# Seven block products in place of eight, extended from seven gate and up blocks to an eighth and to part of the down projection

## The chip, the core and the metric

The kernel runs on one core of a Trainium2 chip. The core has five engines that run side by side and wait for each other through semaphores: TensorE (PE in the profile; its weight loads are PEld), VectorE (DVE), ScalarE (ACT), GpSimd (POOL) and SyncE (SP), which issues most of the transfers from HBM. The metric is the device time of one execution in microseconds (us). What must be the same after a change is the output, within the reference's tolerance; weights come in float32.

## The reference, cut to what matters

256 tokens of width 2048 pass one layer: a mixer, a cross-attention to 256 memory tokens, and a feed-forward network of width 5632. The change lies in the last one and in the norm behind it:

```python
def swiglu(h, w_gate, w_up, w_down):
    return (jax.nn.silu(h @ w_gate) * (h @ w_up)) @ w_down
...
        h = h + swiglu(rmsnorm(h, norm_ffn[i]), w_gate[i], w_up[i], w_down[i])
    return rmsnorm(h, norm_final)
```

`w_gate` and `w_up` are 2048 x 5632, `w_down` is 5632 x 2048.

## The kernel before, in words

**Every product is three matmuls.** A float32 operand is split into a high part that TensorE's fp32r format holds exactly and the low rest: `h` is written by a cast on ScalarE (L208), `l` by a subtraction on VectorE (L209). A product is then high x high, low x high (both with the weight's `h`; L282 and L283) and high x low (L286), summed in PSUM. The tokens (or features) are the stationary operand, 128 x 128; the weights stream by, 128 x 512.

**The weights are one long stream.** `stream_plan` lists keys, and each key is a 256 x 512 block of a weight matrix, laid out as 128 x 1024 (two halves of 512 columns, one for each of two feature tiles). `load_to` has SP load the next key into one of six raw buffers `r`; `split_to` makes `h` and `l` (four buffers each); `tok_mm` multiplies. A key used in the plain way ("plain key") is 2 feature tiles x 2 token halves = 4 block products of three matmuls: 12 matmuls, first eight with `h`, then four with `l`. `unit` sets the order written by hand on PE and SP: it loads up to six keys ahead, splits up to three ahead, runs the matmuls, and appends a list of generators (`post`) that evacuate and go on step by step. VectorE, ScalarE and GpSimd are ordered by the tile scheduler.

**Gate and up, in 11 column blocks of 512** (`ffn_units`). Block 0, and blocks 8 to 10, use the plain way. In blocks 1 to 7 (`SEVEN`) two of the eight key pairs, ("g", n, c) and ("u", n, c) with c of 0 and 1, are multiplied together: two feature tiles by two token halves on one side, two feature tiles by gate and up columns on the other are a 2 x 2 by 2 x 2 block product. Done plainly that is eight block products; `seven_mm` does it with seven (Winograd's form), 21 matmuls in place of 24. It needs

- sums of weight blocks, `pair_sums`: four additions on VectorE in float32 (L182 to L185) and then the split of three new blocks of 128 x 512 (cast L189, subtraction L190);
- sums of token blocks, `token_sums`, made once for c of 0 and 1 and used by all seven blocks;
- four extra PSUM accumulators `p` (tag `m`), whose results `p_post` combines into four corrections (L1080 to L1083), and which `whole` adds to the gate and up accumulators (tag `a`, L1094).

`g_post` applies SiLU on ScalarE, `u_post` multiplies (L1111), transposes (L301) and takes the block through DRAM and back (`put`, `get`, both on SP's queue), after which it is split and kept in `gs` as the features of the down projection. There are 22 such feature pairs, two tiles of 128 each.

**The down projection** takes the four output column blocks n in turn, each with 22 plain keys ("d", n, c). The last two keys of a block (four of the last) are ordered by token half, so that `d_evac` (L1208 and L1211) on the first half runs beside the matmuls of the second.

**Buffers**: `slot` has 63 buffers of 128 x 512 for whatever lives long; `tmp` eight of 128 x 256; `feat` (tag `f`) three of 128 x 1024, used by `get` and `p_post`; `gate` four of 128 x 512.

Of the kernel before, what the change touches and what calls it, by code (L numbers as in the profile page):

```python
# [28 lines left out]
SEVEN = range(1, 8)  # L30
# [55 lines left out]
def ffn_order():  # L86

    return [k for u in ffn_units() for part in u for k in part]


def stream_plan():
# [8 lines left out]
    p += [(k, 1024) for k in ffn_order()]  # L100
    for n in range(4):
        p += [(("d", n, c), 1024) for c in range(FT // 2)]
# [3 lines left out]
def trunk(tc, wst, vecs, xp, xtp, mp, mtp, wdt_in, nfin, outp):  # L106
# [9 lines left out]
    with ExitStack() as ctx:  # L116
# [57 lines left out]
        pairs = {k for u in ffn_units() for part in u if len(part) == 2 for k in part}  # L174

        def pair_sums(nc_, u):


            g = held.pop(nc_)
# [6 lines left out]
            pair_parts[nc_] = []  # L186
            for x in (f[:, a], f[:, b], g[:, a]):
                h, l = slot(dt=F32R), slot(dt=F32R)
                nc.scalar.copy(h, x)  # L189
                tt(l, x, h.bitcast(F32), ALU.subtract)  # L190
                pair_parts[nc_].append((h, l))

        def split_to(n):
            while nsplit[0] < min(n, len(plan)):
# [3 lines left out]
                if key in pairs:  # L198
                    if key[0] == "g":
                        held[key[1:]] = r  # L200
                    else:
                        pair_sums(key[1:], r)
# [872 lines left out]
        def p_post(n, p):  # L1075
# [9 lines left out]
                       ("u", 0): (c12, ALU.add), ("u", 1): (c22, ALU.add)}  # L1085
            return
# [40 lines left out]
        def token_sums(c):  # L1127

            s0, s1 = h2g[2 * c], h2g[2 * c + 1]
            x, y = slot(), slot()  # L1130
            for i, a in enumerate((s0, s1)):
                tt(x[:, i * T:i * T + T], a[:, 0:T].bitcast(F32), a[:, T:].bitcast(F32), ALU.add)
            a11, a21, a12, a22 = [x[:, i * 128:i * 128 + 128] for i in range(4)]
            o = [y[:, i * 128:i * 128 + 128] for i in range(4)]
# [4 lines left out]
            h, l = slot(dt=F32R), slot(dt=F32R)  # L1139
            nc.scalar.copy(h, y)  # L1140
            tt(l, y, h.bitcast(F32), ALU.subtract)
            seven_a[c] = [(h[:, i * 128:i * 128 + 128], l[:, i * 128:i * 128 + 128]) for i in range(4)]

        def seven_mm(n, c):

            g, u, p = faccs["g", n], faccs["u", n], shared[n]
            gh, gl = fin(("g", n, c))
            uh, ul = fin(("u", n, c))
            t1, t2, t4 = pair_parts.pop((n, c))
            a, b = slice(0, 512), slice(512, 1024)  # L1150
            raw = side_blocks(h2g, 2 * c)
            sa = seven_a[c]
            for group in (((p[0], raw(0, 0), (gh[:, a], gl[:, a])), (g[0], raw(1, 0), (gh[:, b], gl[:, b]))),
                          ((p[3], sa[2], (uh[:, a], ul[:, a])), (p[1], sa[0], t1)),
                          ((p[2], sa[1], t2), (g[1], raw(1, 1), t4), (u[0], sa[3], (uh[:, b], ul[:, b])))):
                for ps, (ah, al), (bh, bl) in group:
                    mm(ps, ah, bh, start=c == 0, stop=False)  # L1157
                    mm(ps, al, bh, start=False, stop=False)  # L1158
                for ps, (ah, al), (bh, bl) in group:
                    mm(ps, ah, bl, start=False, stop=c == 1 and any(ps is q for q in p))  # L1160

        def part_mm(part):
            m, n, c = part[0]
            if len(part) == 2:
                seven_mm(n, c)
# [6 lines left out]
        for i, parts in enumerate(ffn_units()):  # L1172
            if i == 8:
                for c in range(2):
                    token_sums(c)
# [26 lines left out]
        for n in range(4):  # L1202
            before.setdefault(index[("d", 0, 8 + 2 * n)], []).append(lambda n=n: load_gain(n))

        def d_evac(n, tb, ps):
# [3 lines left out]
            j = slot()  # L1209
# [12 lines left out]
        def d_sums(tb, ps):  # L1222
            h, j = res[tb][3], slot()
# [58 lines left out]
        nd = FT // 2  # L1282
        for n in range(4):
            accs = [acc(), acc()]
            nt = 2 if n < 3 else 4
            for c in range(0, nd - nt, 2):
                unit([([("d", n, k)], lambda k=k: d_mm(accs, ("d", n, k), (0, 1), k == 0, False))
                      for k in (c, c + 1)])
            tail = [("d", n, k) for k in range(nd - nt, nd)]

            def last_mm(tb):
# [141 lines left out]
```

## Time and profile before

| | |
|---|---|
| median of 3 runs | 1500.95 us (1500.62 to 1501.08) |
| the profiled execution: its time, and the span from its first to its last instruction | 1500.12 us, 1498.4 us |
| busy, share of the span: PE, PEld, DVE, ACT, POOL | 99%, 82%, 68%, 53%, 2% |
| mean granted TensorE clock | 0.998 |
| DMA, mean over the span | 231 GB/s |

The profiled execution's time holds 1.72 us around its span, and it lies 0.83 us below the median of the runs. A row of the timeline gives the start, the length, the engine, the source line, the operation, the tiles (written <- read) and in brackets how long the engine had been idle and what ended that. Lengths of instructions that follow each other overlap, above all on PE, so that the distance between two starts is what an instruction takes of a full engine.

### The profile page before, as it was taken

How to read it: one execution, taken by the hardware profiler on the slowest of the kernel's cores; microseconds unless marked ns; L12 is line 12 of the kernel's file. 1: busy time of each engine (PE TensorE's matmuls, PEld its weight loads, DVE VectorE, ACT ScalarE, POOL GpSimd, SP SyncE). 2: the span in 40 equal slices, each digit the busy share in tenths (PEclk: the TensorE clock that was granted, in tenths of full speed). 3: DMA queues.
4: the chain of work that ended last, by engine and by line, in shares of the span. 5: the costliest groups of instructions: out<-in, count | busy, mean ns of one | idle time of the engine just before them, and what ended most of it. 6: DMA issues, size and time to landing. Idle time of an engine off the chain costs nothing.

```text
span 1498.4 us, 18385 instructions
## 1 busy us (share of the span) xinstructions
PE 1488.0 (99%) x6691; PEld 1226.5 (82%) x6691; DVE 1016.0 (68%) x1320; ACT 796.3 (53%) x1084; POOL 35.3 (2%) x46
## 2 busy tenths in 40 slices
PE   9999999999999999999999999999999999999997
PEld 7788888888888888888888888888888888888886
DVE  6677676777785765665578888888875555445453
ACT  7477554857654544555465555555554444444343
POOL 0011000101000000000000000000000000000000
PEclk9999999999999999999999999999999999999999
DMA  9786766868766766876656766666567667566652
GB/s 367 264 292 224 270 234 212 291 220 291 265 215 240 253 212 210 279 263 207 249 183 228 245 231 225 222 225 223 207 217 243 221 225 248 187 197 196 196 192 90
DMA packets 149211, 346.69 MB, mean 231 GB/s; under 512 B 11360, under 2 KB 62976, under 8 KB 149120
## 3 DMA queue, kind: packets, MB, share of 16 engines
q1 hardware_dynamic: 140064, 338.64, 65.7%
q10 hardware_dynamic: 9056, 6.87, 1.5%
q8 instruction: 52, 0.85, 0.2%
q14 instruction: 39, 0.32, 0.1%
HBM read 321.30 MB, written 24.17 MB: 231 GB/s over the span
## 4 chain that ended last, share of the span: by engine, by line
PE 99%; issue 0%; DMA 0%; SPq 0%; ACT 0%; DVE 0%; DVEq 0%; POOLq 0%; POOL 0%
PE a L282 30%; PE a L283 30%; PE a L286 30%; PE m L1157 1%; PE m L1160 1%; PE m L1158 1%; PE a L1158 1%; PE a L1160 1%; PE a L1157 1%; PE m L703 1%; PE m L283 0%; PE m L286 0%; PE m L282 0%; DMA r<-in_w_dram 0%; PE m L1010 0%
## 5 line engine op out<-in xcount | busy, mean ns | idle before, releaser
L209 DVE TENSOR_TENSOR l<-r,h 128x1024 fp32r<-128x1024 f32 (+1 forms) x539 | 653.6, 1219 | 365.0 <-ACT h L208 355.6
L208 ACT CAST h<-r 128x1024 fp32r<-128x1024 f32 (+1 forms) x539 | 563.1, 1048 | 546.7 <-PE a L283 456.3
L282 PE MATMUL a<-h,s 128*128 128x512 f32 x1999 | 781.9, 391 | 0.2 <-ACT h L208 0.2
L283 PE MATMUL a<-h,s 128*128 128x512 f32 x1999 | 778.1, 389 | 0.0
L286 PE MATMUL a<-l,s 128*128 128x512 f32 x1999 | 538.0, 389 | 0.0
L282 PEld LDWEIGHTS a<-h,s 128*128 128x128 f32 x1999 | 375.4, 188 | 80.2 <-issue 2.0
L286 PEld LDWEIGHTS a<-l,s 128*128 128x128 f32 x1999 | 375.2, 188 | 78.2
L283 PEld LDWEIGHTS a<-h,s 128*128 128x128 f32 x1999 | 375.4, 188 | 77.0
L301 DVE STREAM_TRANSPOSE b<-s 128x512 f32<-128x512 f32 x62 | 40.6, 689 | 6.7 <-ACT s L308 6.7
L644 DVE SCALAR_TENSOR_TENSOR t<-t,vec,t 128x255 f32<-128x255 f32 (+2 forms) x72 | 33.1, 491 | 4.2 <-ACT t L641 3.5
L308 ACT ACTIVATE s<-a,xr 128x512 f32<-128x512 f32 x42 | 26.4, 681 | 4.0 <-PE a L286 4.0
L1094 DVE TENSOR_TENSOR f<-a,f 128x512 f32<-128x512 f32 x28 | 18.0, 684 | 7.8 <-PE a L286 7.8
L1121 ACT CAST s<-f 128x512 fp32r<-128x512 f32 x22 | 13.2, 619 | 14.9 <-DMA f<-w 14.9
L189 ACT CAST s<-b 128x512 fp32r<-128x512 f32 x28 | 16.7, 617 | 4.5 <-DVE b L182 3.6
L190 DVE TENSOR_TENSOR s<-b,s 128x512 fp32r<-128x512 f32 x28 | 18.7, 684 | 0.0
L223 DVE SCALAR_TENSOR_TENSOR s<-s,vec,s 128x256 fp32r<-128x256 f32 x32 | 14.5, 480 | 5.5 <-ACT s L222 5.5
L1233 POOL TENSOR_TENSOR fr<-fr,half 128x1 f32<-128x1 f32 x2 | 1.1, 552 | 704.9 <-DVE fr L1232 704.9
L1122 DVE TENSOR_TENSOR s<-f,s 128x512 fp32r<-128x512 f32 x22 | 14.9, 687 | 3.9 <-ACT s L1121 3.0
L182 DVE TENSOR_TENSOR b<-r,r 128x512 f32<-128x512 f32 x14 | 9.7, 690 | 11.0 <-DMA r<-in_w_dram 11.0
L262 POOL TENSOR_TENSOR rr<-rv,half 128x2 f32<-128x2 f32 x8 | 6.5, 813 | 409.6 <-DVE rv L261 409.6
L626 ACT ACTIVATE s<-s,nacs 128x256 f32<-128x256 f32 x32 | 16.1, 502 | 0.0
L222 ACT ACTIVATE s<-s,vec 128x256 fp32r<-128x256 f32 x32 | 15.2, 502 | 0.8 <-DMA vec<-in_v_dram 0.6
(218 smaller groups left out, 774.9 us busy)
## 6 DMA issues: line engine op xcount, KB each, us to landing
r<-in_w_dram SPq DMA_DIRECT2D x535, 512.0 KB, 4.4
w<-b SPq DMA_DIRECT2D x42, 512.0 KB, 3.3
f<-w SPq DMA_DIRECT2D x42, 512.0 KB, 5.0
s<-acsT ACTq DMA_DIRECT2D x24, 256.0 KB, 4.9
s<-in_xt_dram SPq DMA_DIRECT2D x16, 256.0 KB, 7.2
s<-in_mt_dram SPq DMA_DIRECT2D x8, 256.0 KB, 6.3
s<-in_m_dram SPq DMA_DIRECT2D x8, 256.0 KB, 4.2
s<-in_x_dram SPq DMA_DIRECT2D x7, 256.0 KB, 7.4
```

The lines of the kernel that those rows point to most:

```text
L190: tt(l, x, h.bitcast(F32), ALU.subtract)
L208: nc.scalar.copy(h[:, c], r[:, c])
L209: tt(l[:, c], r[:, c], h[:, c].bitcast(F32), ALU.subtract)
L282: mm(ps[tb], ah, h[:, w], start=first and i == ks[0], stop=False)
L283: mm(ps[tb], al, h[:, w], start=False, stop=False)
L286: mm(ps[tb], blocks(i, tb)[0], l[:, i * 512:i * 512 + 512], start=False, stop=stop and i == ks[-1])
L301: nc.vector.transpose(t[:, tb * 512:tb * 512 + 512], src[tb])
L308: act(o[tb], accs[tb], AF.Identity, scale=r[:, tb:tb + 1])
L644: stt(a[:, d:], u[:, 0:T - d], v("cw", 4 * ct + k), a[:, d:], ALU.mult, ALU.add)
L1157: mm(ps, ah, bh, start=c == 0, stop=False)
L1158: mm(ps, al, bh, start=False, stop=False)
L1160: mm(ps, ah, bl, start=False, stop=c == 1 and any(ps is q for q in p))
```

## The change

`SEVEN` now runs to block 8. In the down projection two column blocks, n and n + 1, are taken together, first 0 and 1, then 2 and 3: the keys ("d", n, c) and ("d", n + 1, c) of the feature pairs c of 0 to 5 are multiplied by `seven_mm`, with the features of pair c as the one side and the two column blocks as the other; the other 16 feature pairs stay plain. Between the pairs stand plain keys by the list `GAPS`: two ahead of the first pair, then 4, 5, 4, 5 and 4. The token sums of a feature pair are made for each of the two column pairs anew, now with buffers of `feat` and `tmp` in place of `slot`. The corrections of the down projection are added to the residual stream in `p_post`. The scratch of the squares (`j`) goes from `slot` to `gate`, and the four loads of the last norm's gain move by one key.

The diff, cut to its core (what is renamed only, and how one function hands its arguments to the next, is left out):

```diff
-SEVEN = range(1, 8)
+SEVEN = range(1, 9)
+GAPS = (2, 4, 5, 4, 5, 4)
...
+def down_units():
+    o = []
+    for n in (0, 2):
+        q = len(GAPS)
+        plain = [("d", n + i, c) for i in range(2) for c in range(q, FT // 2)]
+        tail = 2 if n == 0 else 4
+        for c, k in enumerate(GAPS):
+            o += [[(a,) for a in plain[i:min(i + 2, k)]] for i in range(0, k, 2)]
+            del plain[:k]
+            o.append([(("d", n, c), ("d", n + 1, c))])
+        o += [[(a,) for a in plain[i:min(i + 2, len(plain) - tail)]] for i in range(0, len(plain) - tail, 2)]
+        o.append([(a,) for a in plain[-tail:]])
+    return o
...
-        def p_post(n, p):
+        def p_post(n, p, first=None):
...
+            if n == "d":
+                for i, m in enumerate("gu"):
+                    for tb in range(2):
+                        c, op = corr[n][m, tb]
+                        h = res[tb][first + i]
+                        tt(h, h, c, op)
...
-        def token_sums(c):
-            s0, s1 = h2g[2 * c], h2g[2 * c + 1]
-            x, y = slot(), slot()
-            for i, a in enumerate((s0, s1)):
-                tt(x[:, i * T:i * T + T], a[:, 0:T].bitcast(F32), a[:, T:].bitcast(F32), ALU.add)
...
+        def token_sums(key, parts):
+            xy = fp.tile([128, 1024], F32, tag="f", name=nm("f"))
+            w = 512 // len(parts)
+            for i, (hi, lo) in enumerate(parts):
+                tt(xy[:, i * w:i * w + w], hi.bitcast(F32), lo.bitcast(F32), ALU.add)
+            a11, a21, a12, a22, *o = [xy[:, i * 128:i * 128 + 128] for i in range(8)]
             tt(o[0], a21, a22, ALU.subtract)
             tt(o[1], a11, o[0], ALU.subtract)
             tt(o[2], a21, a11, ALU.subtract)
             tt(o[3], a12, o[1], ALU.subtract)
-            h, l = slot(dt=F32R), slot(dt=F32R)
-            nc.scalar.copy(h, y)
-            tt(l, y, h.bitcast(F32), ALU.subtract)
...
+            for i in range(2):
+                h, l = [tp.tile([128, T], F32R, tag="t", name=nm("t")) for _ in range(2)]
+                y = xy[:, 512 + i * T:512 + i * T + T]
+                nc.scalar.copy(h, y)
+                tt(l, y, h.bitcast(F32), ALU.subtract)
...
         for i, parts in enumerate(ffn_units()):
+            if i == len(ffn_units()) - 3:
+                token_sums(("d", 0, 0), [gs[0]])
...
-            j = slot()
+            j = gtp.tile([128, 512], F32, tag="g", name=nm("j"))
...
-        for n in range(4):
-            accs = [acc(), acc()]
-            nt = 2 if n < 3 else 4
-            for c in range(0, nd - nt, 2):
-                unit([([("d", n, k)], lambda k=k: d_mm(accs, ("d", n, k), (0, 1), k == 0, False))
-                      for k in (c, c + 1)])
...
+        for i, parts in enumerate(units):
+            for key in sums_at.get(i, []):
+                token_sums(key, [gs[key[2]]])
...
+            if len(parts[0]) == 2:
+                _, n, c = keys[0]
+                if c == 0:
+                    shared["d", n] = [msc() for _ in range(4)]
+                if c == len(GAPS) - 1:
+                    post = [p_post("d", shared["d", n], n), d_post(n, daccs[n])]
```

The changed file's lines stand 16 to 26 further down: the split of a key is L224 (cast) and L225 (subtraction) there, the sums of weight blocks L199 to L202 with the splits L206 and L207, `u_post` L1133 and the transposes L317, the matmuls of a plain key L298, L299 and L302, those of `seven_mm` L1179, L1180 and L1182, the token sums L1155 to L1160 with the splits L1165 and L1166, and `d_evac` L1234 and L1237.

Three places show how the orders change. On **TensorE** in the down projection, one plain key of column block 0 before (12 rows for 4 block products: `a_10758` and `a_10759` are the two token halves), and of the change the last 9 of the 21 rows of a pair (c of 1, column blocks 0 and 1; `m_` is an accumulator of `p`, `t_` a token sum, `s_11011` to `s_11020` are weight sums, `s_7487` and `s_7488` the high and low features):

```order
L282 MATMUL a_10758<-h_10857,s_8545 128x512
L283 MATMUL a_10758<-h_10857,s_8546 128x512
L282 MATMUL a_10759<-h_10857,s_8545 128x512
L283 MATMUL a_10759<-h_10857,s_8546 128x512
L282 MATMUL a_10758<-h_10857,s_8545 128x512
L283 MATMUL a_10758<-h_10857,s_8546 128x512
L282 MATMUL a_10759<-h_10857,s_8545 128x512
L283 MATMUL a_10759<-h_10857,s_8546 128x512
L286 MATMUL a_10758<-l_10858,s_8545 128x512
L286 MATMUL a_10759<-l_10858,s_8545 128x512
L286 MATMUL a_10758<-l_10858,s_8545 128x512
L286 MATMUL a_10759<-l_10858,s_8545 128x512
```

The rows of the change are these:

```order
L1179 MATMUL m_10887<-s_11015,t_10932 128x512
L1180 MATMUL m_10887<-s_11015,t_10933 128x512
L1179 MATMUL a_10822<-s_11019,s_7487 128x512
L1180 MATMUL a_10822<-s_11019,s_7488 128x512
L1179 MATMUL a_10883<-h_11023,t_10936 128x512
L1180 MATMUL a_10883<-h_11023,t_10937 128x512
L1182 MATMUL m_10887<-s_11016,t_10932 128x512
L1182 MATMUL a_10822<-s_11020,s_7487 128x512
L1182 MATMUL a_10883<-l_11024,t_10936 128x512
```

Two plain keys (24 matmuls) have become one pair with 21, three for each of seven block products, and the pair reads weight sums and token sums beside the keys themselves. Over the whole program the change has 42 matmuls fewer: 3 for each of 14 pairs, two in block 8 and twelve in the down projection.

On **VectorE** at the seam between gate and up and the down projection, before (`l_10780` to `l_10822` are splits of plain keys; `g_10621` and `g_10623` the last gate and up block, `b_10776` its transpose):

```order
L209 TENSOR_TENSOR l_10780<-r_10717,h_10779 128x1024
L1111 SCALAR_TENSOR_TENSOR g_10621<-a_10605,fscale,g_10621 128x512
L1111 SCALAR_TENSOR_TENSOR g_10623<-a_10606,fscale,g_10623 128x512
L301 STREAM_TRANSPOSE b_10776<-g_10621 128x512
L301 STREAM_TRANSPOSE b_10776<-g_10623 128x512
L209 TENSOR_TENSOR l_10784<-r_10719,h_10783 128x1024
L209 TENSOR_TENSOR l_10818<-r_10753,h_10817 128x1024
L209 TENSOR_TENSOR l_10822<-r_10760,h_10821 128x1024
```

And of the change, at the same place (`l_10801` is the second plain key ahead of the first pair, `r_10780` and `r_10782` are the raw keys of that pair, `l_10845` and `l_10866` their splits):

```order
L225 TENSOR_TENSOR l_10845<-r_10780,h_10844 128x1024
L1133 SCALAR_TENSOR_TENSOR g_10670<-a_10654,fscale,g_10670 128x512
L1133 SCALAR_TENSOR_TENSOR g_10672<-a_10655,fscale,g_10672 128x512
L317 STREAM_TRANSPOSE b_10841<-g_10670 128x512
L317 STREAM_TRANSPOSE b_10841<-g_10672 128x512
L199 TENSOR_TENSOR b_10848<-r_10780,r_10782 128x512
L200 TENSOR_TENSOR r_10782<-r_10782 128x512
L201 TENSOR_TENSOR b_10848<-b_10848,r_10782 128x512
L207 TENSOR_TENSOR s_10854<-b_10848,s_10853 128x512
L202 TENSOR_TENSOR r_10780<-b_10848,r_10780 128x512
L207 TENSOR_TENSOR s_10858<-b_10848,s_10857 128x512
L225 TENSOR_TENSOR l_10866<-r_10782,h_10865 128x1024
```

The sums of the first pair now stand behind `u_post` and ahead of the split of the pair's second key.

On **SP** at the start of the feed-forward network, where the features come back from DRAM (`w_7100` is the last quarter of them, `f_7174` before and `f_7180` now its buffer; the brackets name the semaphores that the issue waits for, DMAHW of a transfer, DVE of VectorE), before:

```order
L321 DMA f_7098<-w_7060 128x8x128 [waits DMAHW4_49,DMAHW1_49]
L314 DMA w_7100<-b_6969 128x2x512 [waits DMAHW5_49]
L169 DMA r_7106<-in_w_dram 128x1024 [waits DMAHW6_49,DVE_49]
L169 DMA r_7136<-in_w_dram 128x1024 [waits DMAHW7_49,DVE_49]
L321 DMA f_7174<-w_7100 128x8x128 [waits DMAHW5_49,DMAHW0_49]
```

And of the change:

```order
L337 DMA f_7098<-w_7060 128x8x128 [waits DMAHW4_49,DMAHW1_49]
L330 DMA w_7100<-b_6969 128x2x512 [waits DMAHW5_49]
L185 DMA r_7106<-in_w_dram 128x1024 [waits DMAHW6_49,DVE_49]
L185 DMA r_7136<-in_w_dram 128x1024 [waits DMAHW7_49,DVE_49]
L337 DMA f_7180<-w_7100 128x8x128 [waits DMAHW4_49,DMAHW5_49,DMAHW0_49,DVE_49]
```

Since two of the three `feat` buffers hold token sums there, the last get now waits for the buffer of the third quarter, `f_7098`: for the last of the four scalings that read it on VectorE.

109 lines of the change are left out of this document (66 added, 43 removed).

## The prediction, written before the result was known

> **What bounds the kernel now.** I read the page first, then who made TensorE wait, then the timeline of one pair that exists already.
>
> ```profile
> span 1498.4 us, 18385 instructions
> ...
> PE 1488.0 (99%) x6691; PEld 1226.5 (82%) x6691; DVE 1016.0 (68%) x1320; ACT 796.3 (53%) x1084; POOL 35.3 (2%) x46
> ...
> PEclk9999999999999999999999999999999999999999
> ...
> PE 99%; issue 0%; DMA 0%; SPq 0%; ACT 0%; DVE 0%; DVEq 0%; POOLq 0%; POOL 0%
> ```
>
> ```profile
> PE m L416 <- POOL U L412: 1.8, 1, 1.8
> PE a L282 <- ACT h L208: 0.2, 1, 0.2
> ```
>
> The chain that ended last is 99% TensorE, and the list of TensorE's waits has two lines, both at the start (2.0 us in all). From then on TensorE runs without a gap and at the full granted clock. So a matmul removed anywhere is worth its distance to the next one, as long as no wait takes its place; and everything that the change adds stands on other engines. Part 1 is the price of a matmul, part 2 whether VectorE, ScalarE and SP can still feed TensorE.
>
> ```profile
> 824.71 0.39 PE L1157 MATMUL m<-h,s 128*128 128x512 f32 x1
> 824.93 0.39 PE L1158 MATMUL m<-h,s 128*128 128x512 f32 x1
> ...
> 829.24 0.39 PE L1160 MATMUL a<-l,s 128*128 128x512 f32 x1
> 829.47 0.39 PE L282 MATMUL a<-h,s 128*128 128x512 f32 x1
> ...
> 831.28 1.07 PE L286 MATMUL a<-l,s 128*128 128x512 f32 x4
> 832.19 0.39 PE L282 MATMUL a<-h,s 128*128 128x512 f32 x1
> ```
>
> Not the 0.39 counts but the distance of starts. A pair (21 matmuls) takes 829.47 - 824.71 = 4.76 us, a plain key (12) 832.19 - 829.47 = 2.72 us; both are 0.2267 us a matmul, whichever mix of PSUM banks and weight sums they use.
>
> **The sum on TensorE.** A pair replaces two plain keys: 2 x 2.72 - 4.76 = 0.68 us. Fourteen pairs are new (two in block 8, twelve in the down projection): 14 x 0.68 = 9.52 us. The change adds no other matmul, transpose or weight load. The Trainium skill's page "TensorE: Matmul & The Clock Gate" (section "Wait — 56ns, not 53.3ns?") gives 215.7 ns between starts at 512 columns and full clock, by which the 42 matmuls would be worth 9.06 us; this trace's own starts are 5% further apart, and I go by the trace.
>
> **VectorE in block 8.** It takes over what blocks 1 to 7 do. The first row is most of these seven, the second the down projection; TensorE waits in neither:
>
> ```profile
> 824.70:1140.00 315.30, 315.30 (x1393) 261.07 (x1391) 260.92 (x315) 166.81 (x196) 0.00 (x0) 1.00 0.66 229
> 1250.00:1480.00 230.00, 230.00 (x1017) 190.44 (x1015) 114.86 (x105) 93.91 (x99) 0.00 (x0) 1.00 0.59 192
> ```
>
> The third and fifth numbers are PE and DVE busy: DVE 83% in the first, 50% in the second, with TensorE at 100% in both. Block 8 costs nothing; its cover is the cover that blocks 1 to 7 have.
>
> **VectorE in the down projection.** Durations from the group list of the first stretch, one row of the page for ScalarE, and one token sum:
>
> ```profile
> L209 DVE TENSOR_TENSOR l<-r,h 128x1024 fp32r<-128x1024 f32 x120 | 144.9, 1217 | 27.0 <-ACT h L208 26.9
> L190 DVE TENSOR_TENSOR s<-b,s 128x512 fp32r<-128x512 f32 x26 | 17.3, 684 | 0.0
> L182 DVE TENSOR_TENSOR b<-r,r 128x512 f32<-128x512 f32 x13 | 9.0, 690 | 10.0 <-DMA r<-in_w_dram 10.0
> ```
>
> ```profile
> L189 ACT CAST s<-b 128x512 fp32r<-128x512 f32 x28 | 16.7, 617 | 4.5 <-DVE b L182 3.6
> ```
>
> ```profile
> 799.88 0.42 DVE L1132 TENSOR_TENSOR s<-s 128x256 f32<-128x256 f32 x1
> ...
> 800.42 0.28 DVE L1135 TENSOR_TENSOR s<-s 128x128 f32<-128x128 f32 x1
> 800.74 0.29 DVE L1136 TENSOR_TENSOR s<-s,s 128x128 f32<-128x128 f32 x1
> ```
>
> A down pair needs two splits (2 x 1.22), seven operations on 128 x 512 (7 x 0.69) and the token sum (one of 0.69, four of 0.29, two of 128 x 256 at 0.42): 2.44 + 4.83 + 2.69 = 9.96 us. With the four plain keys ahead of it (4.88) that is 14.84 us against TensorE's 4 x 2.72 + 4.76 = 15.64; with five, 16.06 against 18.36. So VectorE is at 87 to 95% in these stretches, more than anywhere before, but under TensorE. This counts durations that overlap: 128 x 512 operations start 0.61 us apart (836.07 and 836.68 below). ScalarE has six casts of 1.06 (below), three of 0.62 and two of 128 x 256, some 0.5 each (a quarter of the 1.72 below): 9.2 us in the 15.64. What matters beside the mean is how late VectorE may be:
>
> ```profile
> 1225.20 1.06 ACT L208 CAST h<-r 128x1024 fp32r<-128x1024 f32 x1 [1.66 <-PE a L283]
> ```
>
> ```profile
> 1226.29 1.23 DVE L209 TENSOR_TENSOR l<-r,h 128x1024 fp32r<-128x1024 f32 x1 [1.50 <-ACT h L208]
> ```
>
> ```profile
> 1234.07 0.39 PE L282 MATMUL a<-h,s 128*128 128x512 f32 x1
> ...
> 1235.88 0.39 PE L286 MATMUL a<-l,s 128*128 128x512 f32 x1
> ```
>
> With plain keys, the cast at 1225.20 waits for TensorE to free one of four `h` buffers, and its split at 1226.29 ends at 1227.52; that key's turn comes at 1234.07, and its `l` is first read at 1235.88. The lead is 8.4 us. A pair's extra VectorE work, 4.83 + 2.69 = 7.5 us, fits into it once, and the spare time of the plain keys restores it.
>
> Where two such loads meet I added up the queue by hand. **The seam to the down projection** (second order in the section on the change): from the end E of the last gate and up matmul, VectorE has `u_post`, the transposes and the sums of the first pair ahead of the split `l_10866`.
>
> ```profile
> 1206.84 1.41 DVE L1111 SCALAR_TENSOR_TENSOR g<-a,fscale,g 128x512 f32<-128x512 f32 x2 [1.09 <-PE a L286]
> 1208.16 1.29 DVE L301 STREAM_TRANSPOSE b<-g 128x512 f32<-128x512 f32 x2
> 1209.38 2.31 DVE L209 TENSOR_TENSOR l<-r,h 128x1024 fp32r<-128x1024 f32 x2
> ```
>
> ```profile
> 835.34 0.69 DVE L182 TENSOR_TENSOR b<-r,r 128x512 f32<-128x512 f32 x1 [1.55 <-DMA r<-in_w_dram]
> 836.07 0.69 DVE L183 TENSOR_TENSOR r<-r 128x512 f32<-128x512 f32 x1
> 836.68 0.68 DVE L184 TENSOR_TENSOR b<-b,r 128x512 f32<-128x512 f32 x1
> ```
>
> ```profile
> 1206.87 0.39 PE L282 MATMUL a<-h,s 128*128 128x512 f32 x1
> ```
>
> In block 9 `u_post` starts as TensorE goes on to the next block (1206.84 and 1206.87), so E is its start, and what follows the transposes starts 1209.38 - 1206.84 = 2.54 us after E. Six operations at 0.61 to 0.73 and the split of 1.22 end at E + 2.54 + 3.7 + 1.2 = E + 7.4. TensorE wants it after two plain keys, the pair's first six matmuls and four of its second group: E + 5.44 + 10 x 0.2267 = E + 7.7. That is a margin of 0.3 us. Bounds: a cost of 0 if the rows hold (there is no wait to gain from), and 1.5 us if each of the six operations takes 0.73 in place of 0.61 and one cast of 1.06 comes late, less the margin. I take 0.2, near the lower end, since the same operations ran in that pitch above.
>
> **Behind the last pair of a column pair** stand `p_post`, four additions to the residual stream and `d_evac`: 11 to 12 operations of 0.69 us, 8 us, ahead of the split of the fourth key. They can start in the pair's last group, 0.5 us before its end, and TensorE has three split keys (8.16 us) and that key's eight first matmuls (1.81) until it needs the split, which ends 8.7 us after the pair: margin 1.2 us, cost 0. The accumulators of the pairs and of block n are next needed eight keys later (21.8 us); those of block n + 1 two keys and 18 matmuls after its last one (9.5 us), with four operations of `d_evac` before that. Both cost 0.
>
> **SP.** The last get of the features now waits for VectorE's scaling of the third quarter:
>
> ```profile
> 789.09 0.39 SPq L321 DMA_DIRECT2D f<-w  x1
> ...
> 797.35 0.38 SPq L321 DMA_DIRECT2D f<-w  x1
> ```
>
> ```profile
> f<-w SPq DMA_DIRECT2D x42, 512.0 KB, 5.0
> ```
>
> ```profile
> 796.60 1.69 DVE L860 SCALAR_TENSOR_TENSOR s<-f,vec,s 128x256 fp32r<-128x256 f32 x4 [2.88 <-ACT s L859]
> ```
>
> ```profile
> 796.05 1.72 ACT L859 ACTIVATE s<-f,vec 128x256 fp32r<-128x256 f32 x4 [3.60 <-DMA f<-w]
> ...
> 806.40 1.71 ACT L859 ACTIVATE s<-f,vec 128x256 fp32r<-128x256 f32 x4
> ```
>
> The scalings end at 796.60 + 1.69 = 798.3, so the get goes out 0.95 us later than at 797.35, with the raw keys behind it on the queue. Block 0 has 16 keys before 824.71, so it starts at 781.2 and needs these features at its eleventh key, 808.4. Before, they were scaled from 806.40 on, because ScalarE was busy. If the get takes the median of 5.0 us, or the 7.0 between the issue before it (789.09) and its reader (796.05), it lands at 803.3 to 805.3: hidden. The raw keys behind it are six deep. Cost 0; up to 2 us if it is later than that. The other loads keep their bytes: two keys in 4.76 us are 220 GB/s, where the first stretch ran at 229. The gain's loads wait on buffers that the gate and up matmuls have freed, or the first pair; cost 0.
>
> Sum against the profiled execution: 1500.12 - 9.52 + 0.2 = 1490.8 us. The median of the runs shown is 0.83 above that execution, so the median to expect is **1491.6 us**, 0.6% less.
>
> **The rivals.**
> - *All hidden* (my forecast): 1491.0 to 1492.3 us. For it: seven blocks with the same chunks and no wait. Chance 0.66.
> - *Short waits in the down projection*: at the seam, or where a weight sum that a pair needs last stands behind the split of a later key on the in-order engines. One cast (1.06) or split (1.23) of lateness in one to three places: 1 to 3.5 us, 1492.3 to 1495. Chance 0.19.
> - *The late features* at the start of the network: 1.5 to 3 us, 1493 to 1494.6. Against it the three microseconds until 808.4. Chance 0.06.
> - *The other side: VectorE becomes the bound in the pair stretches.* My 14.84 us leaves 0.80 of 15.64. If the hand-overs with ScalarE cost waits of 4.8 us in each stretch (12 of them at 0.4, a quarter of the 1.50 that the split at 1226.29 sat idle for its cast), VectorE needs 19.64, TensorE waits 4.0 in each of ten stretches, less the lead of 8.4 once in each column pair: 40 - 16.8 = 23 us, 1515. It decides against the change from 2.6 us of overload a stretch ((9.52 + 16.8) / 10), 3.4 us of waits. Against it: the 27.0 us idle ahead of 120 splits above were spent with buffers full, not late. Chance 0.04.
> - *Loads late*, because a pair holds two raw buffers until its last weight sum: 4 to 8 us over twelve pairs, 1495 to 1499. Against it: the first stretch holds them too. Chance 0.05.
> - That the change doesn't do what it says is excluded by the order, which has 42 matmuls fewer.
>
> The same Trainium skill page says that ScalarE's and VectorE's queues are strictly first in, first out (section "Architectural detail: the array is 16× 32×32, not 1× 128×128"). That rule is what would make the fourth case bite; no row here shows an engine held up by it.
>
> **How the numbers follow.** 1490.6 to 1495.0 takes in the first three cases, a little below the first for the spread of runs (0.3 us): 0.9 of the chance, less what may lie outside their bounds. The likeliest case alone is 1491.0 to 1492.3. About 0.2% (3 us) can be told from no change: faster below 1497.95 takes the first three and half of the loads' case, 0.93; within 0.2% 0.03; slower 0.04.
>
> **What the profile of the changed kernel would show.** If I am right: 42 PE instructions fewer (6649) and PE busy near 1478.5 us; the list of TensorE's waits as short as before; a pair of the down projection 4.76 us long; DVE busy up by about 14 x 4.83 + 12 x 2.69 + 24 x 0.69 = 116 us (weight sums, token sums, and 8 operations of 0.69 in block 8 and behind each column pair), to 1132; ScalarE's by some 40. If waits replaced matmuls, L298 or L1182 stands in that list with VectorE as releaser, at the seam or from the second pair on; loads late would show as waits of L224 or L199 on `r`; late features as L298 waiting near 808. Wrong I would be if the span fell by less than 7 us.

## The result, and the profile after

The changed kernel takes 1491.3 us (median of four runs, 1491.18 to 1491.33) against 1500.82 us of the kernel before on the same chip: ratio 0.9936, 95% interval 0.9919 to 0.9954. The forecast was 1491.6.

The page of the changed kernel (busy times per engine, then the shares of the chain that ended last), and its list of TensorE's waits:

```profile
span 1489.6 us, 18607 instructions
...
PE 1478.4 (99%) x6649; PEld 1218.6 (82%) x6649; DVE 1109.9 (75%) x1528; ACT 829.6 (56%) x1155; POOL 34.4 (2%) x46
...
PE 98%; DMA 0%; issue 0%; SPq 0%; ACT 0%; DVE 0%; DVEq 0%; POOLq 0%; POOL 0%
```

```profile
PE m L432 <- POOL U L428: 1.8, 1, 1.8
PE a L298 <- ACT h L224: 1.0, 1, 1.0
```

TensorE has its 42 instructions fewer and is 9.6 us less busy; the span fell by 8.8 us. The list of waits is still two lines, both at the program's start. The second was 0.2 us before and 1.0 now. That is scatter of the start: it was between 0 and 0.9 us in the experiments below too, also where nothing early was changed. So I read small differences from the long stretch behind it, from the first pair of block 1 to the last matmul of the program. Of the changed kernel these are the first row and the last of the following; the two rows between them are the first matmuls of two neighbouring pairs of the down projection:

```profile
825.37 0.39 PE L1179 MATMUL m<-h,s 128*128 128x512 f32 x1
...
1289.18 0.39 PE L1179 MATMUL m<-h,s 128*128 128x512 f32 x1
...
1304.83 0.39 PE L1179 MATMUL m<-h,s 128*128 128x512 f32 x1
...
1480.86 0.28 PE L1306 MATMUL a<-h,s 128*128 128x256 f32 x1
```

The same last matmul of the kernel before, whose first pair started at 824.71:

```profile
1489.66 0.28 PE L1280 MATMUL a<-h,s 128*128 128x256 f32 x1
```

This long stretch took 664.95 us before and takes 655.49 now, 9.46 less where 42 x 0.2267 = 9.52 were removed. A pair and four plain keys, a stretch in the prediction's sense, take 1304.83 - 1289.18 = 15.65 us, so a down pair is 4.77 us long, where 4.76 was forecast.

The seam to the down projection, in the timeline (start, duration, engine, line, idle time before and what ended it):

```profile
1249.67 1.41 DVE L1133 SCALAR_TENSOR_TENSOR g<-a,fscale,g 128x512 f32<-128x512 f32 x2 [1.09 <-PE a L302]
1250.99 1.29 DVE L317 STREAM_TRANSPOSE b<-g 128x512 f32<-128x512 f32 x2
1252.21 0.65 DVE L199 TENSOR_TENSOR b<-r,r 128x512 f32<-128x512 f32 x1
1252.89 0.63 ACT L206 CAST s<-b 128x512 fp32r<-128x512 f32 x1 [5.57 <-DVE b L199]
1252.89 0.69 DVE L200 TENSOR_TENSOR r<-r 128x512 f32<-128x512 f32 x1
...
1253.75 1.05 ACT L224 CAST h<-r 128x1024 fp32r<-128x1024 f32 x1 [0.23 <-DVE r L200]
...
1255.96 1.22 DVE L225 TENSOR_TENSOR l<-r,h 128x1024 fp32r<-128x1024 f32 x1
```

```profile
1249.69 0.39 PE L298 MATMUL a<-h,s 128*128 128x512 f32 x1
...
1257.40 0.40 PE L1182 MATMUL m<-l,t 128*128 128x512 f32 x1
```

The split of the first pair's second half ends at 1257.18 and is read at 1257.40: 0.22 us to spare. VectorE in three windows behind it; the first begins at the end of the first pair, and each ends 2 us behind the next pair (length; then PE, PEld, DVE, ACT, POOL busy; granted clock, DMA share, GB/s at the end):

```profile
1259.95:1277.56 17.61, 17.61 (x79) 14.61 (x78) 17.17 (x30) 9.71 (x14) 0.00 (x0) 1.00 0.94 309
1277.56:1295.92 18.36, 18.36 (x83) 15.21 (x82) 17.92 (x30) 11.47 (x15) 0.00 (x0) 1.00 0.65 224
1295.92:1311.56 15.64, 15.64 (x71) 12.95 (x70) 13.12 (x17) 9.02 (x11) 0.00 (x0) 1.00 0.67 230
```

VectorE comes out of the seam with nothing in hand, works 98% of the time in two windows until it is ahead again, and then needs 84%.

### The profile page after: what moved, and what is told of

The parts are those of the page before. It is cut to its first block, busy times and chain, and to the rows that moved or that the text cites. A ratio compares the mean times of both kernels' runs of the same rounds, so it can differ in the third digit from the quotient of the medians.

```text
span 1489.6 us, 18607 instructions
## 1 busy us (share of the span) xinstructions
PE 1478.4 (99%) x6649; PEld 1218.6 (82%) x6649; DVE 1109.9 (75%) x1528; ACT 829.6 (56%) x1155; POOL 34.4 (2%) x46
## 4 chain that ended last, share of the span: by engine, by line
PE 98%; DMA 0%; issue 0%; SPq 0%; ACT 0%; DVE 0%; DVEq 0%; POOLq 0%; POOL 0%
PE a L298 29%; PE a L299 29%; PE a L302 29%; PE m L1182 2%; PE m L1180 2%; PE m L1179 2%; PE a L1179 1%; PE a L1182 1%; PE a L1180 1%; PE m L719 1%; PE m L299 0%; PE m L298 0%; PE m L302 0%; DMA r<-in_w_dram 0%; PE m L1026 0%
## 5 line engine op out<-in xcount | busy, mean ns | idle before, releaser
L225 DVE TENSOR_TENSOR l<-r,h 128x1024 fp32r<-128x1024 f32 (+1 forms) x539 | 652.4, 1218 | 262.3 <-ACT h L224 253.0
L224 ACT CAST h<-r 128x1024 fp32r<-128x1024 f32 (+1 forms) x539 | 563.4, 1049 | 488.1 <-PE a L299 349.3
L298 PE MATMUL a<-h,s 128*128 128x512 f32 x1887 | 738.2, 391 | 1.0 <-ACT h L224 1.0
L299 PE MATMUL a<-h,s 128*128 128x512 f32 x1887 | 734.5, 389 | 0.0
L302 PE MATMUL a<-l,s 128*128 128x512 f32 x1887 | 507.4, 389 | 0.0
L298 PEld LDWEIGHTS a<-h,s 128*128 128x128 f32 x1887 | 354.3, 188 | 76.5 <-ACT h L224 2.1
L302 PEld LDWEIGHTS a<-l,s 128*128 128x128 f32 x1887 | 354.2, 188 | 73.8
L299 PEld LDWEIGHTS a<-h,s 128*128 128x128 f32 x1887 | 354.4, 188 | 72.6
L206 ACT CAST s<-b 128x512 fp32r<-128x512 f32 x56 | 33.9, 619 | 21.0 <-DVE b L199 17.2
L317 DVE STREAM_TRANSPOSE b<-s 128x512 f32<-128x512 f32 x62 | 40.6, 690 | 6.4 <-ACT s L324 6.4
L207 DVE TENSOR_TENSOR s<-b,s 128x512 fp32r<-128x512 f32 x56 | 37.9, 687 | 0.0
L199 DVE TENSOR_TENSOR b<-r,r 128x512 f32<-128x512 f32 x28 | 19.3, 689 | 17.3 <-DMA r<-in_w_dram 17.2
L1182 PE MATMUL m<-s,t 128*128 128x512 f32 x56 | 21.8, 389 | 0.0
L1179 PE MATMUL m<-s,t 128*128 128x512 f32 x56 | 21.8, 389 | 0.0
L1180 PE MATMUL m<-s,t 128*128 128x512 f32 x56 | 21.8, 389 | 0.0
L206 ACT CAST s<-r 128x512 fp32r<-128x512 f32 x28 | 17.3, 619 | 6.5 <-DVE r L202 6.3
L200 DVE TENSOR_TENSOR r<-r 128x512 f32<-128x512 f32 x28 | 19.3, 689 | 0.4
L207 DVE TENSOR_TENSOR s<-r,s 128x512 fp32r<-128x512 f32 x28 | 19.2, 686 | 0.4 <-ACT s L206 0.4
```

The source lines that it names most:

```text
L224: nc.scalar.copy(h[:, c], r[:, c])
L225: tt(l[:, c], r[:, c], h[:, c].bitcast(F32), ALU.subtract)
L298: mm(ps[tb], ah, h[:, w], start=first and i == ks[0], stop=False)
L299: mm(ps[tb], al, h[:, w], start=False, stop=False)
L302: mm(ps[tb], blocks(i, tb)[0], l[:, i * 512:i * 512 + 512], start=False, stop=stop and i == ks[-1])
L317: nc.vector.transpose(t[:, tb * 512:tb * 512 + 512], src[tb])
```

## The experiments

All times are medians against the kernel before on the same chip (1500.6 to 1501.0 us). Runs of one kernel scatter by up to a few microseconds, so what is smaller is read from the long stretch defined above, which took 655.49 us in the changed kernel.

| kernel | time, us | ratio, 95% interval | long stretch, us | against the changed kernel |
|---|---|---|---|---|
| 42 matmuls left out | 1491.28 | 0.9935 (0.9922 to 0.9948) | 655.43 | -0.06 |
| block 8 alone | 1499.21 | 0.9988 (0.9979 to 0.9997) | 663.61 | +8.12 |
| down projection alone | 1492.44 | 0.9942 (0.9928 to 0.9956) | 656.86 | +1.37 |
| seam four operations later | 1494.08 | 0.9957 (0.9944 to 0.9970) | 658.32 | +2.83 |
| four more a pair | 1491.84 (one run) | | 656.27 | +0.78 |
| eight more a pair | 1518.64 (one run) | | 682.86 | +27.37 |
| eight pairs, gaps of 3 | 1490.19 | 0.9930 (0.9912 to 0.9948) | 654.53 | -0.96 |
| blocks 9 and 10 too | 1491.65 | 0.9939 (0.9923 to 0.9955) | 654.71 | -0.78 |
| eight pairs by the lead | 1488.85 | 0.9922 (0.9910 to 0.9935) | 652.96 | -2.53 |
| eight pairs by the lead, and blocks 9 and 10 too | 1487.12 | 0.9908 (0.9893 to 0.9923) | 651.08 | -4.41 |
| the same with 65 buffers | 1486.07 | 0.9904 (0.9890 to 0.9917) | 650.31 | -5.18 |

### What the matmuls alone are worth

```diff
 (kernel before)
-                    mm(ps[tb], al, h[:, w], start=False, stop=False)
+                    if not less or i == 0:
+                        mm(ps[tb], al, h[:, w], start=False, stop=False)
...
+            tok_mm(..., less=key[1] == 1 and key[2] < 20 or key[1:] == (2, 5))
```

> The kernel before, with 42 matmuls of the down projection left out and nothing else (21 keys without the product of the activations' low parts with the second 128 rows of the weights; so the output lacks these small terms). It is the price of 42 matmuls with no other work added. Theory (a matmul is worth its 0.2267 us and all else that the change adds is hidden but for about 0.06 us at the seam): 1500.82 - 9.52 = 1491.30 us, within 0.15 of the changed kernel's 1491.30. Rival (the change has hidden costs of its own, for instance 0.5 to 1 us of short hand-overs that no row names): this kernel ends 0.5 to 1 us below the changed one, at 1490.3 to 1490.8. Rival (a matmul is worth 215.7 ns, by the Trainium skill's page TensorE: Matmul & The Clock Gate): 1491.76.

1491.28 us, a ratio of 0.9935 where the changed kernel has 0.9936. From its first pair's first matmul to its last:

```profile
825.39 0.39 PE L1158 MATMUL m<-h,s 128*128 128x512 f32 x1
...
1480.82 0.28 PE L1281 MATMUL a<-h,s 128*128 128x256 f32 x1
```

That is 655.43 us, 9.52 less than before: 42 x 0.2267 to the hundredth. The changed kernel needs 0.06 more. So everything that it adds, 94 us of VectorE and 33 of ScalarE, costs 0.06 us. The rival with hidden costs of half a microsecond falls. The price from the Trainium skill's page "TensorE: Matmul & The Clock Gate" (section "Wait — 56ns, not 53.3ns?"), 215.7 ns a matmul, would have given an estimated 9.06 us in this stretch; the trace has 9.52.

### The two parts apart

```diff
 (kernel before, block 8 alone)
-SEVEN = range(1, 8)
+SEVEN = range(1, 9)
```

> Only the first part of the change: the kernel before with block 8 as a seven-product block, the down projection plain. Theory: two pairs of 0.68 us, 1500.82 - 1.36 = 1499.46 us, no new line among TensorE's waits. Rival (block 8 costs something, since its weight sums and corrections stand late on VectorE): between 1499.5 and 1500.8, with a wait of L209 or the weight sums there.

```diff
 (changed kernel, down projection alone)
-SEVEN = range(1, 9)
+SEVEN = range(1, 8)
```

> Only the second part: the changed kernel with block 8 left plain. Theory: twelve pairs of 0.68 us, 1500.82 - 8.16 = 1492.66 us, so that the two parts add up to the whole. Rival (the parts share a cost, for instance the seam or the late features): the two gains together differ from 9.52 us by 0.3 us or more.

The timed gains, 1.75 and 8.52 us against the 1500.96 us of the kernel before beside them, add up to 0.7 more than 9.52, by which the rival would be right. Block 8 alone ran from 1498.67 to 1500.18 though, and the traces don't have this difference. Block 8 alone:

```profile
824.91 0.39 PE L1157 MATMUL m<-h,s 128*128 128x512 f32 x1
...
1488.52 0.28 PE L1280 MATMUL a<-h,s 128*128 128x256 f32 x1
```

663.61 us, 1.34 less than before; the down projection alone 656.86, 8.09 less. Together 9.43, against 9.46 for both at once. They are additive, and neither has a wait of its own in the list.

### The seam's margin

```diff
 (changed kernel, in pair_sums)
-            tt(f[:, a], g[:, a], u[:, a], ALU.add)
+            for _ in range(5 if key == ("d", 0, 0) else 1):
+                tt(f[:, a], g[:, a], u[:, a], ALU.add)
```

> The changed kernel with the first weight sum of the first down pair done five times in place of once (the same values): four more VectorE operations of 0.61 us, 2.44 us, in the queue right behind u_post's transposes and ahead of the split that the first pair's second half needs. Theory (that split ends 0.22 us before TensorE reads it, and nothing else gives way): TensorE waits 2.44 - 0.22 = 2.2 us at L1183, 1493.5 us; the keys behind it are then two microseconds later on TensorE too, so nothing more is lost. Rival (the margin is larger than the trace's 0.22 us, since the wait for that split could be on the cast or another hand-over): 1491.3 to 1492.3. Rival (the lateness is passed on through the next stretches, where VectorE is at 97% until the third pair): 1494.5 to 1496.

+2.8 us. TensorE's waits and the seam's timeline (in this kernel and the next two, lines are one further down):

```profile
PE m L1183 <- DVE l L226: 1.2, 1, 1.2
PE m L1180 <- ACT h L225: 1.1, 1, 1.1
```

```profile
1252.15 3.55 DVE L200 TENSOR_TENSOR b<-r,r 128x512 f32<-128x512 f32 x5
...
1255.74 0.62 ACT L207 CAST s<-b 128x512 fp32r<-128x512 f32 x1 [8.48 <-DVE b L200]
1255.74 0.69 DVE L201 TENSOR_TENSOR r<-r 128x512 f32<-128x512 f32 x1
...
1256.60 1.05 ACT L225 CAST h<-r 128x1024 fp32r<-128x1024 f32 x1 [0.24 <-PE a L1183]
...
1257.69 0.50 PE L1180 MATMUL m<-h,t 128*128 128x512 f32 x1 [1.10 <-ACT h L225]
1258.03 0.40 PE L1181 MATMUL m<-h,t 128*128 128x512 f32 x1
...
1260.08 0.50 PE L1183 MATMUL m<-l,t 128*128 128x512 f32 x1 [1.19 <-DVE l L226]
```

The named waits are 2.3 us, where 2.2 were expected, but that agreement is luck, for two errors cancel. From the first addition to L201 the five take 3.59 us (1252.15 to 1255.74), the one of the changed kernel 0.68: the four added ones are worth 2.91 us, 0.73 each, not the 0.61 that I had taken. Less the margin of 0.22 that is 2.7 us, and 2.83 are lost. So the margin is real to about 0.1 us, and nothing else gives way. The list names 0.5 us less than is lost: after a wait the first matmul stands 0.34 from the next in place of 0.23, and the wait begins 0.16 us before the profile counts it. A wait of TensorE costs some 0.3 us more than the list says.

Half of the named waits already falls on the cast of the pair's second half, which comes 2.85 us later (1256.60; 1253.75 in the changed kernel). Its row names a matmul as what ended its wait (it started at 1256.20), but in the changed kernel the cast ran 2.5 us before that matmul. It also reads the sum of L201, which ends at 1256.43, and in both kernels it starts 0.17 us behind the end of that sum. So its lateness is that of VectorE's sums.

Two of the five runs took 1495.73 and 1495.94 us, which is within the third expectation, at a mean granted clock of 0.997; the other three took 1493.76 to 1494.08 at 0.998. The trace is of one of these three. The 1.7 us between them are what 3.5 us at half clock, as in the next section, would cost; no trace shows whether that is it.

### How much VectorE can take

```diff
 (changed kernel, in pair_sums; 5 and 9)
-            tt(f[:, a], g[:, a], u[:, a], ALU.add)
+            for _ in range(5 if key[0] == "d" and key[2] else 1):
+                tt(f[:, a], g[:, a], u[:, a], ALU.add)
```

> The changed kernel, where in the down projection each pair but the first of each column pair does its first weight sum five times (the same values): 4 more VectorE operations of 0.61 us, 2.44 us a pair, 12.2 us in the five stretches of a column pair. From the end of the first pair to the end of the sixth TensorE takes 3 x 15.64 + 2 x 18.36 = 83.64 us. Theory (VectorE's need is its busy time in the changed kernel's trace, 73 us in these stretches with the catching up from the seam, some 70 without): 82 us still fit, no wait inside the stretches; but the lead of 8.4 us isn't regained, so that the 12 operations behind the last pair come late: 0 to 5 us a column pair, 1491.3 to 1501. Rival (the sum of single durations that I predicted with, 14.84 and 16.06 us a stretch, is the need): 76.6 + 13 = 89.6 us, 6 us of waits inside the stretches of each column pair as well: 1503 or more.

1491.84 us, half a microsecond more. One new wait, at the second pair, which comes before VectorE has regained its lead. VectorE's windows behind it show it full, and then 95% busy; no further wait is listed:

```profile
PE m L1183 <- DVE l L226: 0.5, 1, 0.5
```

```profile
1277.56:1295.92 18.36, 18.36 (x83) 15.20 (x82) 18.36 (x32) 10.15 (x14) 0.00 (x0) 1.00 0.56 197
...
1329.92:1345.56 15.64, 15.64 (x71) 12.95 (x70) 14.88 (x19) 8.15 (x10) 0.00 (x0) 1.00 0.52 182
```

By single durations a stretch of four keys and a pair would have needed 14.84 + 2.6 = 17.4 us of 15.64, and the kernel should have slowed to 1503. VectorE's busy time, in which durations that overlap count once, is the better measure, but not an exact one. The added operations start 0.72 us apart where they follow each other, not 0.61; the 20 of a column pair are then 14.4 us, with the 70 to 73 of the expectation more than the 83.64 that there are, and still only one wait comes of it. DVE busy rises by no more than 21.3 us (1131.2 against 1109.9) for all 40. Why isn't shown. The 12 operations behind the last pair made no wait.

> As the kernel with four more operations a pair, with eight: 24.4 us more VectorE work in the five stretches of a column pair. Theory (need by busy time): 94 us against 83.64, 10.6 us of waits in each column pair, and the operations behind the last pair on top, 4 to 6 us each: 1521 to 1526 us, slower than the kernel before. Rival (need by single durations): 102.6 against 83.64, 19 us each, and the same on top: 1537 to 1542. Rival (the lead of 8.4 us is there from the first pair on, as my fourth rival had it): 1496 to 1500.

1518.64 us: slower than the kernel before, and nearest to the first expectation. The lead is used up at the seam, so the third falls. The first was 2 to 7 us too high: it had 4 to 6 us behind the last pair of each column pair, and no wait is listed there. The waits at the pairs are some 24 us with the slower starts behind them, where it had 21 for both column pairs. The list, and eight of the nine additions of one pair merged into a row, 0.72 us apart:

```profile
PE m L1183 <- DVE l L226: 10.2, 10, 1.2
PE m L1180 <- ACT h L225: 7.9, 6, 2.5
...
1344.23 5.77 DVE L200 TENSOR_TENSOR b<-r,r 128x512 f32<-128x512 f32 x8
```

18.1 us of named waits stand against 27.4 us lost. 16 waits at 0.3 us more each, as above, are some 5. Most of the rest is in two places like this one, rows and a window of the same time (granted clock third from the end):

```profile
1274.78 0.50 PE L1180 MATMUL m<-h,t 128*128 128x512 f32 x1 [2.53 <-ACT h L225]
...
1277.17 0.76 PE L1183 MATMUL m<-l,t 128*128 128x512 f32 x1 [1.19 <-DVE l L226]
...
1278.15 0.63 PE L1180 MATMUL m<-s,t 128*128 128x512 f32 x1
1278.58 0.63 PE L1181 MATMUL m<-s,t 128*128 128x512 f32 x1
...
1280.69 0.39 PE L1183 MATMUL m<-s,t 128*128 128x512 f32 x1
```

```profile
1278.00:1280.00 2.00, 2.00 (x6) 1.52 (x6) 2.00 (x3) 0.61 (x1) 0.00 (x0) 0.50 0.89 277
```

Behind the waits the granted clock is 0.50 and matmuls start 0.43 us apart, for 3.5 us. It happens twice (again at 1444), some 1.7 us each. About 1 us in all is spread over delays too short for the list.

### More pairs: where the room is

```diff
-GAPS = (2, 4, 5, 4, 5, 4)
+GAPS = (2, 3, 3, 3, 3, 3, 3, 3)
```

(Here and in the other kernels with other gaps the gain's loads are tied to keys 12, 14, 16 and 18 in place of 9 to 15.)

> The changed kernel with eight pairs in each column pair in place of six, three plain keys between them in place of four and five. On TensorE 4 x 0.68 = 2.72 us less. A stretch is then 3 x 2.72 + 4.76 = 12.92 us. Theory (VectorE's need is its busy time, 0.91 of the single durations' 13.62, so 12.4 us): no wait inside the stretches, 1488.6 us; but the lead is regained by only half a microsecond a stretch, so that the operations behind the last pair may cost up to 4 us in each column pair: 1488.6 to 1496. Rival (need by single durations, 13.62): 0.7 x 7 = 4.9 us of waits in each column pair besides, 1498 or more, most of the change's gain lost.

1490.19 us, in the theory's range: of the 2.72 us, 0.96 arrive in the long stretch. TensorE's waits behind the start, and VectorE from the end of the first pair to almost the end of the eighth:

```profile
PE m L1182 <- DVE s L207: 0.6, 1, 0.6
PE m L1182 <- DVE l L225: 0.2, 1, 0.2
```

```profile
1259.60:1350.00 90.40, 89.79 (x396) 73.67 (x395) 85.33 (x131) 52.29 (x71) 0.00 (x0) 1.00 0.67 230
```

85.33 us, where seven stretches by single durations are 7 x 13.62 = 95.3 us: the rival falls once more. The waits stand at the second pair of each column pair (1271.11 and 1372.74 on the timeline), at the end of the first gap of 3, while VectorE is still catching up. The pairs stand 13.98 and 13.38 us apart there, and 12.92 elsewhere, so 1.5 us are lost at two places. Behind the last pair, where I had put up to 4 us a column pair, 0.2 are lost, and only in the second: two matmuls, at 1473.62 and 1473.96, start 0.34 us behind the one before, which is too short for the list. So the range was met, but not in the way that the theory had it.

```diff
-SEVEN = range(1, 9)
+SEVEN = range(1, 11)
```

> The changed kernel with seven products in blocks 9 and 10 too, so in all gate and up blocks but block 0. On TensorE four pairs, 2.72 us less. Since block 10 then has its own corrections, two more operations of 0.65 us stand ahead of u_post, and with it ahead of the seam's weight sums. Theory (the seam's margin of 0.2 us is the narrow place): 1.1 us of waits at the first down pair and some 0.3 us of slower starts behind them, 1490.0 us. Rival (the buffers for the features and for the weight sums run out, as blocks 9 and 10 hold the most gated features): waits in blocks 9 and 10 of a microsecond or more, 1491 to 1500. Rival (all hidden): 1488.6.

The median of 1491.65 us has four runs from 1490.21 to 1492.46 in it, and its profiled run reached block 1 at 827.13, 1.8 us later than the changed kernel's; the stretch is 0.78 us shorter, not 2.72. Both the theory and the rival on buffers are seen:

```profile
PE m L1182 <- DVE l L225: 0.9, 1, 0.9
...
PE a L1179 <- ACT s L206: 0.3, 1, 0.3
```

```profile
1188.41 0.62 ACT L206 CAST s<-r 128x512 fp32r<-128x512 f32 x1 [0.28 <-PE m L1182]
```

The first is the seam, 1.1 us with the slower starts. The second is in block 9's second pair: the cast of its third weight sum starts only when TensorE has read something, which I took to be the last reader of the buffer that it writes; 0.7 us are lost there.

### Placing the pairs by the lead

```diff
-GAPS = (2, 4, 5, 4, 5, 4)
+GAPS = (4, 4, 3, 3, 3, 2, 2, 2)
```

> Eight pairs in each column pair again, with the plain keys between them placed by the lead: four ahead of the first pair (two before), then gaps of 4, 3, 3, 3, 2, 2, 2 in place of seven gaps of 3. TensorE's work is that of the kernel with eight pairs and gaps of 3. Theory (that kernel lost 1.5 us since VectorE came out of the seam without a lead and its second pair followed three keys on; two more plain keys at the seam give 2 x (2.72 - 1.22) = 3.0 us of lead, the gap of 4 some 2 more, and the gaps of 2, in which VectorE needs some 11.1 us of TensorE's 10.20, eat 0.9 each): no wait at the second pair, 1488.6 us. Rival (VectorE's capacity over the whole column pair is what lacks, 94 to 98% busy there): waits of 1 to 3 us at the last pairs or behind them, 1489.6 to 1491.6. Rival (as many as eight pairs cost the same wherever they stand): 1490.2.

1488.85 us; as many pairs as with gaps of 3, 1.57 us less in the stretch. The first three pairs:

```profile
1260.40 0.39 PE L1179 MATMUL m<-h,s 128*128 128x512 f32 x1
...
1276.04 0.39 PE L1179 MATMUL m<-h,s 128*128 128x512 f32 x1
...
1288.96 0.39 PE L1179 MATMUL m<-h,s 128*128 128x512 f32 x1
```

15.64 and 12.92 us, without a loss. It was the lead, not the capacity. What is left of the loss is 0.2 us behind the last pair, as with gaps of 3.

```diff
-SEVEN = range(1, 9)
-GAPS = (2, 4, 5, 4, 5, 4)
+SEVEN = range(1, 11)
+GAPS = (4, 4, 3, 3, 3, 2, 2, 2)
```

> The kernel with eight pairs placed by the lead, and seven products in blocks 9 and 10 as well. TensorE's work is 8 x 0.68 = 5.44 us less than in the changed kernel: 1485.9 us. Theory: two operations more ahead of u_post delay the seam's weight sums by 1.3 us, and this is now covered by two more plain keys (5.44 us), so no wait at the first down pair, where the kernel with blocks 9 and 10 alone lost 1.13 us; in block 9's second pair 0.8 us stay lost, where a weight sum's cast waits for a buffer that TensorE frees: 1486.7. Rival (the seam's wait isn't of the order on VectorE but goes with blocks 9 and 10 however many keys stand ahead): 1487.8 or more.

1487.12 us (1486.32 to 1487.57), 0.4 above the theory's figure and below the rival's 1487.8. The trace decides: the wait at L1182 is gone, and what is left behind the start is block 9's.

```profile
PE a L1179 <- ACT s L206: 0.3, 1, 0.3
```

```diff
 (the kernel above)
-        rawp = E(tc.tile_pool(name="raw", bufs=6))
+        rawp = E(tc.tile_pool(name="raw", bufs=5))
...
-        sp = E(tc.tile_pool(name="slots", bufs=63))
+        sp = E(tc.tile_pool(name="slots", bufs=65))
```

> The same, with two more of the 128 x 512 buffers (65 in place of 63), paid for with one of six raw buffers for weights. Theory (block 9's second pair waits for such buffers): the 0.7 us there go, 1485.9 to 1486.2. Rival (five raw buffers make loads late): waits on raw keys, 1487 or more. Rival (that wait isn't for a buffer): 1486.7, as with 63.

1486.07 us (1485.94 to 1486.75), 5.2 us less than the changed kernel and 14.5 less than before. The wait in block 9 is gone, so it was for a buffer, and five raw buffers make no load late: the list of TensorE's waits has the start's 1.8 us (L432) and no other line. The window from the last keys before the seam on:

```profile
1250.00:1345.00 95.00, 95.00 (x421) 78.71 (x420) 94.08 (x147) 57.06 (x78) 0.00 (x0) 1.00 0.62 215
```

VectorE is at 99% there and TensorE still doesn't wait in that window. By that row a ninth pair would hardly find room, though busy time was no exact measure above; it wasn't run.

## Why the prediction was right, step by step

- *Price of a matmul.* 42 x 0.2267 = 9.52 us: shown by the kernel that only leaves 42 matmuls out.
- *Block 8 at nothing.* 1.34 us of 1.36 arrive alone.
- *The seam.* E + 7.4 for the split and E + 7.7 for its reader were 7.5 and 7.7 (E = 1249.69, where TensorE goes on to the next key). The cost taken was 0.2; it is 0.06. There is no wait; the first pair's last ten matmuls only start 0.23 to 0.24 apart. That the margin is as thin as forecast is shown by the four added operations.
- *VectorE's load.* Right in sign, too high in size. I gave 87 to 95% of a stretch from single durations; it is 84% once the lead is back, and 98% in two windows behind the seam. DVE busy rose by 94 us, not 116, and ScalarE's by 33, not 40, since durations that overlap count once: added up one by one, the durations in the traces rose by 117 and 39. The lead is back by the fourth pair, where ScalarE's cast at 1304.16 again waits 1.67 us for TensorE to free a buffer, but at the first two pairs it isn't there. The fourth rival had it "once in each column pair".
- *That rival itself.* With eight more additions in each stretch, 5.8 us where I had assumed 4.8 of hand-overs, the kernel takes 1518.64 us where I had 1515. The place, at the pairs, was right; that the size comes so near is luck. I had 4.0 us of waits in each of ten stretches, less a lead of 8.4 once in each column pair. Without the halved clock TensorE lost 24 us, 2.4 a stretch, and no lead was there to take off. In the changed kernel itself the overload is missing.
- *Behind the last pair, features, loads.* Cost 0, as taken. Even with four more operations a pair nothing waits behind the last pair, and with eight pairs 0.2 us are lost there. The get of the features goes out at 798.87 and its reader starts at 803.02, before the 803.3 to 805.3 that I gave.
- *"No row here shows an engine held up" by the strict order.* That sentence doesn't hold for the changed kernel: ScalarE stands 5.57 us at the first weight sum's cast at the seam, and 8.48 us with the four added operations, and no later cast overtakes it. The Trainium skill's rule on ScalarE's and VectorE's queues, cited in the prediction, fits both rows. Whether the order itself cost TensorE anything isn't shown: the cast for which it waits there reads a sum of VectorE that is late itself.

## What to carry to other kernels

When TensorE runs without a gap, each matmul removed is worth its distance to the next, and work that is added elsewhere is free as long as its engine keeps up. Busy time with overlaps counted once judged that better here than the sum of single durations, though not exactly. What failed first here was not the mean load but the place where the other engine has no lead, the seam and the first pair behind it: give it easy keys there and pack the pairs densely where it is ahead. A wait found in such a place has two cures to try, the order of the work and one more buffer.

## What the runs showed of the hardware

- Behind two waits of TensorE, 2.53 and 1.19 us with four matmuls between them, the granted clock was 0.50 for 3.5 us (0.43 us a matmul); it was so behind 2.18 and 1.19 too, and stayed at 1.00 behind 1.30 and 1.20 or 1.16 and 1.19. The Trainium skill's page "TensorE: Matmul & The Clock Gate" (section "HAM oscillation — how this bites in real kernels") puts it as no idle gap above some 3.4 us. No single gap here was that long; what the two cases share is 3.4 to 3.7 us of waits close together. The half rate that the same page of the Trainium skill gives, 426.7 ns a matmul (section "Wait — 56ns, not 53.3ns?"), is what the trace has. Where the limit lies, and over what time waits count, stays open: the kernel with the later seam has waits of 1.10 and 1.19 us in its trace without a halved clock, and two of its other runs were longer at a lower mean clock.
- A wait of TensorE costs some 0.3 us beyond its listed length (2.83 us lost for 2.29 listed at the seam). 0.16 of it is how the list counts, from the end of a matmul recorded as 0.39 us long though the next one usually starts 0.23 us behind its start; 0.11 is the later start of the second matmul.
- The same addition done again and again starts 0.72 us apart on VectorE (eight in 5.8 us), while most of the different operations of a pair's weight sums start 0.60 to 0.61 us apart. Why isn't shown.
- The start of the program moves by up to 2.4 us (first pair at 824.71 to 827.13) between profiled runs of kernels whose first 780 us are alike, so a gain of a microsecond is better read from a stretch of the trace behind it.
